# Rolling a matrix in HBM: 16 DMA engines placed 516 rows apart and a 128-column strip, where they stood 4 rows apart with a 256-column strip

## The chip, the cores and the metric

The kernel runs on one core of a Trainium2 chip. That core has 16 DMA engines, which move bytes between HBM and HBM and between HBM and the on-chip memory (SBUF). The metric is the device time of one launch in microseconds (us), given as the median of several runs; lower is better.

## The reference

```
x = np.random.randn(8192, 8192).astype(np.float32)      # 8192 rows of 32 KB
out = np.roll(x, 100, axis=1)
```

Each row is moved 100 columns to the right: `out[r, 100:] = x[r, :8092]`, and the last 100 columns of `x[r]` become `out[r, :100]`. Nothing is computed. All 268.4 MB are read once and written once.

## The kernel before, in words

The output is cut by columns. `s` is the shift, 100. `a` is the width of a strip at the left of the output: the shift rounded up to 128 columns, and then, by a rule of two lines (20 to 22), widened by another 128, so `a` is 256. `g = a - s` is 156: the first column of `x` that the strip does not take.

**The main part** (line 38) is `out[:, 256:] = x[:, 156:8092]`: 7936 columns, or 31,744 bytes of each row, copied from HBM to HBM with no stop on the chip. The rows go in blocks of 64. In block `c` there are four DMAs, `j` = 0 to 3; each has 16 rows, one for each DMA engine, and engine `e` takes row `64c + 4e + j`. So neighbouring engines are always 4 rows (128 KB) apart, all sixteen are in one block of 64 rows (2 MB), and one engine goes by 1 row three times and then 61 rows on, to its place in the next block. The DMAs are issued alternately by SyncE (SP: `j` = 0 and 2) and ScalarE (ACT: `j` = 1 and 3), 256 by each. Four DMAs of each queue are open at a time: the fifth waits until all 16 engines have finished the first.

**The strip** (lines 60 to 77) is the first 256 columns of the output, which cross the end of the rows in `x`. It goes through SBUF, with GpSimd (POOL) as issuer. The rows go in 4 stages of 2048 (`n_st`): 128 partitions of 16 consecutive rows, which are J = 4 groups of Q = 4 rows. Since row `r`'s last 100 columns and row `r+1`'s first columns are neighbours in HBM, one piece of 256 columns (1 KB) fetches both: for `q` = 1 to 3, line 68 reads the piece that begins 100 columns before row `q` of each group into the tile `t`. Line 69 fetches the last 100 columns of the fourth row (400-byte pieces), and line 72 the first 156 columns of the first row (624-byte pieces), straight into the tile `h`. VectorE (DVE) copies the other parts from `t` to `h` (lines 70 and 73). Then line 77 writes `h` out, one DMA for each `q` and stage: 512 pieces of 1 KB. In all there are 20 loads and 16 stores by POOL; eight may be open at a time, and the ninth waits for the first.

There are no waits between the main part and the strip: they share the 16 DMA engines, HBM, and nothing else. The Tile framework sets the semaphores; the order of each queue is that of the program.

Of the kernel before, what the change touches and what calls it, by code (L numbers as in the profile page):

```python
# [1 line left out]

# [4 lines left out]


@with_exitstack
def kernel(  # L10
    ctx: ExitStack,
    tc: tile.TileContext,
    x: bass.AP,
    shift: int,
    out: bass.AP,
):
    nc = tc.nc
    n_rows, n_cols = x.shape
    s = shift % n_cols
    a = -(-s // 128) * 128  # L20
    if 0 < a <= 384 and a + 128 <= n_cols:
        a += 128
    g = a - s
    P = nc.NUM_PARTITIONS
    engines = [nc.sync, nc.scalar]
    n_chunks = 16
    rows = n_rows // n_chunks

    xm = x.rearrange("(c e j) w -> c j e w", e=16, j=4)
    om = out.rearrange("(c e j) w -> c j e w", e=16, j=4)
    if a < n_cols:
        for c in range(n_rows // 64):
            for j in range(4):
                engines[j % 2].dma_start(out=om[c, j, :, a:], in_=xm[c, j, :, g:n_cols - s])
    if a == 0:
        return  # L40


    if a > 512:
        for i in range(n_chunks):
            r = slice(i * rows, (i + 1) * rows)
            nc.gpsimd.dma_start(out=out[r, :s], in_=x[r, n_cols - s:])
            if g > 0:
                nc.gpsimd.dma_start(out=out[r, s:a], in_=x[r, :g])
        return

    Q, J = 4, 4
    n_st = n_rows // (P * Q * J)
    reads = ctx.enter_context(tc.tile_pool(name="reads", bufs=n_st))
    heads = ctx.enter_context(tc.tile_pool(name="heads", bufs=n_st))
    xt = x.rearrange("(k p j q) c -> k q p j c", q=Q, j=J, p=P)
    ot = out.rearrange("(k p j q) c -> k q p j c", q=Q, j=J, p=P)  # L60
    tiles = []
    for k in range(n_st):
        t = reads.tile([P, Q - 1, J, a], x.dtype)
        h = heads.tile([P, Q, J, a], x.dtype)
        for q in range(1, Q):
            lead = bass.AP(tensor=x.tensor, offset=(k * P * J * Q + q) * n_cols - s,
                           ap=[[J * Q * n_cols, P], [Q * n_cols, J], [1, a]])
            nc.gpsimd.dma_start(out=t[:, q - 1], in_=lead)  # L68
        nc.gpsimd.dma_start(out=h[:, Q - 1, :, :s], in_=xt[k, Q - 1, :, :, n_cols - s:])  # L69
        nc.vector.tensor_copy(h[:, :Q - 1, :, :s], t[:, :, :, :s])  # L70
        if g > 0:
            nc.gpsimd.dma_start(out=h[:, 0, :, s:], in_=xt[k, 0, :, :, :g])  # L72
            nc.vector.tensor_copy(h[:, 1:, :, s:], t[:, :, :, s:])  # L73
        tiles.append(h)
    for k, h in enumerate(tiles):
        for q in range(Q):
            nc.gpsimd.dma_start(out=ot[k, q, :, :, :a], in_=h[:, q])  # L77


# [1 line left out]
_INS = ['x', 'shift']  # L81
_OUTS = [((8192, 8192), 'float32')]

_NUMBERS = {'shift': 100}


# [26 lines left out]
```

## Time and profile before

| | |
|---|---|
| median of 3 runs | 819.57 us (819.18 to 820.42) |
| the profiled execution, its own time | 820.42 us |
| its span, first to last instruction | 818.3 us |
| HBM read / written | 268.44 MB / 268.44 MB |
| moved by the DMA engines | 276.89 MB (strip bytes count twice: in and out) |
| main part, two queues | 2 x 130.04 MB |
| strip, one queue | 16.78 MB |
| last strip store issued | at 373.0 us |

In the profile, a DMA's packets carry their own times. For the main part a packet is one row (31,744 bytes), followed by a packet of 4 bytes that counts up a semaphore; so half of the packets of these two queues are rows. A strip packet is some 4 KB and holds several pieces: four of 1 KB, seven of 624 bytes, or ten or eleven of 400 bytes. The share of a queue is the time of its packets as a part of 16 engines' time in the window, so packet time can be had from a share: share x 16 x window / number of rows. Traffic on HBM in a window is twice the bytes of the main queues, which are read and written there, plus the strip queue's bytes, which touch HBM once.

### The profile page before, as it was taken

The page shows a single profiled execution, that of the slowest core. Times are in us where ns is not written, and L with a number is a line of the kernel's source. Part 1 is how long each engine was busy: PE and PEld are TensorE (multiplying, and loading weights), DVE is VectorE, ACT ScalarE, POOL GpSimd, SP SyncE. Part 2 cuts the span into 40 slices and gives each one's busy share as a digit, 9 for nine tenths or more (in the row PEclk, how much of TensorE's full clock was granted, in tenths as well). Part 3 has the DMA queues.
Part 4 walks back from the last instruction along what each step waited for, and adds up shares of the span by engine and source line. Part 5 has one row for each costly group of instructions (what it writes and reads, how often), then busy time and mean ns, then how long its engine had stood idle before and what let it go on. Part 6 is the DMA issues. An engine that isn't in the chain of part 4 may idle for free. (4 is left out here: it accounts for less than half of the span.)

```text
span 818.3 us, 617 instructions
## 1 busy us (share of the span) xinstructions
DVE 7.7 (1%) x8; POOL 28.8 (4%) x40
## 2 busy tenths in 40 slices
DVE  0000000000000000000000000000000000000000
POOL 3000000000000000000000000000000000000000
DMA  9999999999999999999999999999999999999997
GB/s 313 343 345 352 338 352 342 363 338 358 349 342 352 354 355 352 348 364 357 337 335 341 327 335 334 326 332 334 338 337 334 330 334 334 332 327 334 334 321 262
DMA packets 21060, 276.89 MB, mean 338 GB/s; under 512 B 8768, under 2 KB 8768, under 8 KB 12864
## 3 DMA queue, kind: packets, MB, share of 16 engines
q10 hardware_dynamic: 8192, 130.04, 46.4%
q1 hardware_dynamic: 8192, 130.04, 46.0%
q0 software_dynamic: 4672, 16.78, 6.8%
q14 instruction: 4, 0.03, 0.0%
HBM read 268.44 MB, written 268.44 MB: 656 GB/s over the span
## 5 line engine op out<-in xcount | busy, mean ns | idle before, releaser
L77 POOL DMA_DIRECT2D out_dram<-h x16 | 13.2, 825 | 197.8 <-DMA out_dram<-h 112.6
L68 POOL DMA_DIRECT2D t<-in_x_dram x12 | 9.5, 793 | 59.7 <-DMA h<-in_x_dram 30.0
L70 DVE COPY h<-t 128x1200 f32<-128x1200 f32 x4 | 3.1, 786 | 232.3 <-DMA t<-in_x_dram 173.4
L73 DVE COPY h<-t 128x1872 f32<-128x1872 f32 x4 | 4.9, 1224 | 0.0
L69 POOL DMA_DIRECT2D h<-in_x_dram x4 | 3.0, 748 | 45.4 <-DMA t<-in_x_dram 45.4
L72 POOL DMA_DIRECT2D h<-in_x_dram x4 | 3.0, 750 | 41.7 <-DMA t<-in_x_dram 41.7
L94 POOL MEMSET const-float32-0.0<- 128x1 f32 x1 | 0.1, 98 | 0.2 <-issue 0.2
L94 POOL MEMSET const-bfloat16-1.0<- 128x1 bf16 x1 | 0.1, 102 | 0.0
L94 POOL MEMSET const-uint8-127<- 128x1 uint8 x1 | 0.1, 99 | 0.0
L94 POOL MEMSET const-float32-1.0<- 128x1 f32 x1 | 0.1, 98 | 0.0
## 6 DMA issues: line engine op xcount, KB each, us to landing
out_dram<-in_x_dram ACTq DMA_DIRECT2D x256, 496.0 KB, 12.6
out_dram<-in_x_dram SPq DMA_DIRECT2D x256, 496.0 KB, 12.6
out_dram<-h POOLq DMA_DIRECT2D x16, 512.0 KB, 113.7
t<-in_x_dram POOLq DMA_DIRECT2D x12, 512.0 KB, 94.9
h<-in_x_dram POOLq DMA_DIRECT2D x4, 312.0 KB, 92.1
h<-in_x_dram POOLq DMA_DIRECT2D x4, 200.0 KB, 97.4
```

What stands on the lines that cost most here:

```text
L68: nc.gpsimd.dma_start(out=t[:, q - 1], in_=lead)
L69: nc.gpsimd.dma_start(out=h[:, Q - 1, :, :s], in_=xt[k, Q - 1, :, :, n_cols - s:])
L70: nc.vector.tensor_copy(h[:, :Q - 1, :, :s], t[:, :, :, :s])
L72: nc.gpsimd.dma_start(out=h[:, 0, :, s:], in_=xt[k, 0, :, :, :g])
L73: nc.vector.tensor_copy(h[:, 1:, :, s:], t[:, :, :, s:])
L77: nc.gpsimd.dma_start(out=ot[k, q, :, :, :a], in_=h[:, q])
L94: nc = _bacc.Bacc("TRN2", target_bir_lowering=False, num_devices=1)
```

## The change

The strip is 128 columns wide again: the rule of two lines is gone, so `a` = 128 and `g` = 28. J is 8, so the strip has 2 stages of 4096 rows and not 4 of 2048; its pieces are 512 bytes (and 400 and 112 bytes in `h`). The main part has 8064 columns, or 32,256 bytes, of each row.

The main part has a new order. `pitch` is 516 rows, `steps` is 7. A DMA still has 16 rows, one for each engine, but now engine `e` takes row `516e + 4q + 64i + j`. `j` runs fastest (1 row), then `i` from 0 to 6 (64 rows), then `q` from 0 to 15 (4 rows). This makes 448 DMAs. The rows that it leaves over are copied between `q` = 7 and `q` = 8: 60 DMAs of 16 rows that are 4 rows apart, as all were before, four of 15 rows, 516 apart, and four of a single row, which are cut into 16 parts of 504 columns (2016 bytes). That is 516 DMAs, 258 by each queue, where there were 512.

```diff
     a = -(-s // 128) * 128
-    if 0 < a <= 384 and a + 128 <= n_cols:
-        a += 128
     g = a - s
...
-    xm = x.rearrange("(c e j) w -> c j e w", e=16, j=4)
-    om = out.rearrange("(c e j) w -> c j e w", e=16, j=4)
+    pitch, steps = n_rows // 16 + 4, n_rows // 16 // 64 - 1
+    run = steps * 64
+
+    def main(n, first, step, count):
+        o = bass.AP(tensor=out.tensor, offset=first * n_cols + a, ap=[[step * n_cols, count], [1, n_cols - a]])
+        i = bass.AP(tensor=x.tensor, offset=first * n_cols + g, ap=[[step * n_cols, count], [1, n_cols - a]])
+        engines[n % 2].dma_start(out=o, in_=i)
+
     if a < n_cols:
-        for c in range(n_rows // 64):
-            for j in range(4):
-                engines[j % 2].dma_start(out=om[c, j, :, a:], in_=xm[c, j, :, g:n_cols - s])
+        for q in range(16):
+            for i in range(steps):
+                for j in range(4):
+                    main(j, 4 * q + 64 * i + j, pitch, 16)
+            if q == 7:
+                for e in range(15):
+                    for j in range(4):
+                        main(j, pitch * e + run + j, 4, 16)
+                for j in range(4):
+                    main(j, run + 64 + j, pitch, 15)
+                    main(j, n_rows - 4 + j, 1, 1)
...
-    Q, J = 4, 4
+    Q, J = 4, 8
     n_st = n_rows // (P * Q * J)
```

## The prediction

> **What bounds the kernel now.** I read the page's engine shares and DMA slices first, then its queues.
>
> ```profile
> span 818.3 us, 617 instructions
> DVE 7.7 (1%) x8; POOL 28.8 (4%) x40
> ...
> DMA  9999999999999999999999999999999999999997
> ...
> DMA packets 21060, 276.89 MB, mean 338 GB/s; under 512 B 8768, under 2 KB 8768, under 8 KB 12864
> ## 3 DMA queue, kind: packets, MB, share of 16 engines
> q10 hardware_dynamic: 8192, 130.04, 46.4%
> q1 hardware_dynamic: 8192, 130.04, 46.0%
> q0 software_dynamic: 4672, 16.78, 6.8%
> ...
> HBM read 268.44 MB, written 268.44 MB: 656 GB/s over the span
> ```
>
> No compute engine matters. The shares add up to 99.2% of 16 engines: the DMA engines always have a packet open. q10 and q1 are the main part, q0 the strip. A busy engine is not one at its full rate, though, so the next view is SP's own waits.
>
> ```profile
> SPq L38 <- DMA out_dram<-in_x_dram: 670.4, 252, 3.9
> ```
>
> 252 of SP's 256 issues waited, 670 us in all, for one of its four open DMAs. An issue itself takes 0.51 us, or 131 us in all. So the queues wait for the data, not the data for them. Then the DMA view of three stretches: strip loads (20 to 170 us), strip stores (240 to 360), main part alone (500 to 700).
>
> ```profile
> q10 hardware_dynamic: 1464, 23.27, 43.4%
> q1 hardware_dynamic: 1459, 23.11, 41.1%
> q0 software_dynamic: 1637, 5.79, 15.4%
> ```
>
> ```profile
> q1 hardware_dynamic: 1176, 18.67, 44.7%
> q10 hardware_dynamic: 1173, 18.54, 44.5%
> q0 software_dynamic: 1453, 5.28, 11.5%
> ```
>
> ```profile
> q1 hardware_dynamic: 2099, 33.34, 50.4%
> q10 hardware_dynamic: 2101, 33.37, 49.4%
> ```
>
> Bytes first, main part twice. Loads: (2 x 46.38 + 5.79) MB / 150 us = 657 GB/s on HBM. Stores: (2 x 37.21 + 5.28) / 120 = 664. Alone: 2 x 66.71 / 200 = 667. Now the time of one main row: 84.5% of 16 x 150 us over 1461 rows is 1388 ns beside the loads, 89.2% of 16 x 120 us over 1172 rows is 1461 ns beside the stores, and 99.8% of 16 x 200 us over 2101 rows is 1520 ns alone. When strip traffic comes in, main rows get faster by just so much that HBM traffic stays within 1.5%. The trace's fastest rows take 1174 ns, about a quarter of those in the last stretch. So what sets the end is the rate at which HBM serves these sixteen copies, some 667 GB/s, and not the DMA engines' own pace.
>
> **The strip, halved.** Every byte is still read from HBM once and written once: 536.87 MB before and after. What goes is the second handling by a DMA engine: the strip moves 8.39 MB and not 16.78, the main part 264.24 MB and not 260.08. Two ways of pricing that:
>
> By engine time, what the queues were charged is 99.2% of 818.3 us, 811.8 us. Strip: 6.8% of 818.3 is 55.6 us, halved 27.8. Main: 92.4% is 756.1 us; rows of 32,256 bytes for 31,744 add 1.6%, or 12.2. Sum -15.6 us. This end supposes that main rows keep their mean time per byte when the strip shrinks. The stretches show the opposite: without a strip a row takes 1520 ns, not 1388.
>
> By HBM traffic, the strip costs only what HBM loses while it runs. Loads: (667 - 657) / 667 x 150 us is 2.3 us for 5.79 MB, so 3.3 us for all 8.39 MB that are loaded. Stores: (667 - 664) / 667 x 120 us is 0.5 us for 5.28 MB, 0.8 for 8.39; the passage between the two (180 to 240 us, 649 GB/s by the same sum) makes it nearer 1.3. Together 4.6 us, and -2.3 when half of the bytes are gone. The other bound here: the number of pieces stays the same (8192 stored, one for each row, 1 KB before and 512 B after). If the loss goes by pieces, nothing is gained; if a 512-byte piece loses twice what a 1 KB piece does, +4.6. For it stands that the 400-byte pieces' packets took no longer per byte in the load stage than the 1 KB pieces' (284 ns for 4400 bytes, 267 for 4096, between 50 and 100 us of the trace). I take -2.3, by the row that it is nearest to, HBM's traffic; ends -15.6 and +4.6.
>
> POOL issues 10 loads and 8 stores in place of 20 and 16, of the same 512 KB (400 and 112 in `h`). Only two of the loads have to wait for one of the eight slots (12 did). DVE has four copies over 24 rows each for eight over 12. All of it hides: nobody in the main part waits for POOL or DVE, and strip work, of which the last store was issued at 373 us, should be issued by some 190 and landed by 250. If it were not, 550 us of main part are left as cover.
>
> **The new order of rows.** SP and ACT issue 258 DMAs each, +2 x 0.51 us, hidden in the 670 us of waits. The remainder in the middle: four DMAs of 15 rows leave one engine with four rows fewer, and four single rows add a 2016-byte part per engine. Sixteen engines wait for one at most: 4 rows x 1.5 us / 16 is 0.4 us. While these are open, a queue holds two real rows per engine, not four; DMAs land in 12.6 us with four open, so an engine that is 6 us ahead of the last can run dry once. Bound: 0 to 6 us; I take +0.4, since the other engines get HBM's free share.
>
> The spacing is the large unknown. Per engine, the sequence stays: 1, 1, 1, then 61 rows on; only each eighth jump differs. Between engines, 516 rows are 16 MiB + 128 KiB where there were 128 KiB; the 60 DMAs in the middle (12% of the rows) keep 4 rows. Modulo 512 rows the sixteen positions are the same as before. Nothing in this trace shows sixteen main rows 16 MiB apart. The nearest rows are those of the lone main part, a mean of 1520 ns in the 805 us from the first issue to the last. Ends: if all of them ran at the fastest, 1174 ns, the 805 us would be 622, -183 us; if all ran at the trace's 95th percentile, 2030 ns, on the 88% that are moved, +240 us. What the same kernel does from stretch to stretch, 649 to 667, is 2.7%. I take 0, because the positions modulo 512 rows stay, and because engines are not in step today (the first and the last engine of one DMA finish some 6 us apart, four rows), so no fixed pattern between them is there to be broken.
>
> A rule speaks against it: the Trainium skill, "DMA: Bandwidth & Descriptors", section "Latency and other measured facts", has HBM-to-HBM copies at half rate when streams lie 4 or 8 MiB apart, and full rate again with 4 KiB added to the pitch. By the rule without the padding, 88% of the rows at half rate would make some 1530 us; with the 128 KiB counted as padding, no change. No run here shows either. The other way, "HBM Reference", section "Specifications (TRN2)", gives a domain some 716 GB/s; 667 is 93% of that, so by this page even a perfect order would save 7% at most, to about 762 us.
>
> **Sum.** -2.3 + 0.4 = -1.9 us. Against the profiled execution's own 820.42 us (span 818.3 and 2.1 around it) that is 818.5; the median of the runs lies 0.85 below it, so 817.7 us.
>
> **The rivals.**
> 1. The spacing helps. For: three quarters of the lone main rows are slower than 1174 ns, so streams hinder each other, and regions 16 MiB apart may do so less. Against: 667 GB/s is hardly left in any stretch of 50 us (650 to 673). If HBM gains 2%, the 805 us lose 16 and the time is 802 us; at 1%, 810.
> 2. The spacing hurts (the other side). All rows 128 KiB apart lie in one stretch of 2 MB now; sixteen far regions may collide where neighbours did not. 3% on the moved 88% is 0.88 x 805 x 0.03 = 21 us: 839 us. It decides as soon as the mean main row is longer than its scaled 1520 x 1.016 = 1544 ns by 0.5%, at 1552.
> 3. The engines' time counts after all: -15.6 + 0.4, 804 us. For: 99% busy. Against: the rows' 1388, 1461 and 1520 ns.
> 4. 512-byte pieces cost HBM more: +4.6 + 0.4, 824.6 us. Against: the 400-byte packets.
>
> That the change doesn't do what it says, because the remainder's slots or the four-open window keep engines near each other, is out: positions are fixed by the addresses.
>
> **How the numbers follow.** Forecast 0.34, rival 1 0.22, rival 2 0.30, rival 3 0.07, rival 4 0.07. A change of under 0.2% (1.6 us) can't be told from none in this kernel. The forecast's own range is 814 to 820: half of its chance is faster, some 0.12 within 0.2%, 0.05 slower. So faster 0.17 + 0.22 + 0.07 = 0.46, same 0.12, slower 0.05 + 0.30 + 0.07 = 0.42. The range must reach into rivals 1 and 2: from 798 (HBM up by 2.5%) to 844 (3.7% on the moved rows), about one in ten left out on each side.
>
> **What the profile after would show.** Strip: q0 at 8.39 MB, its last store issued before 200 us. Forecast: HBM near 667 GB/s in a stretch of main part alone, rows near 1544 ns. Rival 1: rows below 1530. Rival 2: rows above 1552, and a dip of row time in the middle, where the 60 DMAs are 4 rows apart. Rival 3: rows at 1490 or less with q0 halved. Rival 4: less HBM traffic while the strip runs than 657, the rest unchanged. Wrong in any case if the slices show DMA gaps around the remainder.

## The result, and the profile after

The changed kernel takes 822.84 us (median of 4 runs, 822.02 to 823.95) where the kernel before took 819.38 in the same comparison: a ratio of 1.0043, with a 95% interval of 1.0025 to 1.0062. It is slower by 0.43%, some 3.5 us. The forecast was 817.7 us, faster by 0.23%: the time lies within the stated 798 to 844 us, a range wide enough for either sign, and the sign is wrong. The profiled execution took 822.36 us, with a span of 820.6.

The page of the changed kernel, its DMA slices and queues:

```profile
span 820.6 us, 593 instructions
DVE 3.7 (0%) x4; POOL 16.1 (2%) x22
...
DMA  9999999999999999999999999999999999999997
...
DMA packets 18845, 272.70 MB, mean 332 GB/s; under 512 B 8541, under 2 KB 8605, under 8 KB 10653
## 3 DMA queue, kind: packets, MB, share of 16 engines
q1 hardware_dynamic: 8252, 132.14, 47.6%
q10 hardware_dynamic: 8252, 132.14, 47.0%
q0 software_dynamic: 2336, 8.39, 4.4%
...
HBM read 268.44 MB, written 268.44 MB: 654 GB/s over the span
```

The bytes went as the change says: the strip's queue moves 8.39 MB and not 16.78, all engines together 272.70 MB and not 276.89. It won nothing. The engines are as busy as before and HBM's mean rate fell from 656 to 654 GB/s. This page shows best what kind of kernel it is: 4.2 MB less to move, and more time.

The DMA view of the strip's loads in the changed kernel (20 to 100 us), then of the main part alone (500 to 700 us); columns are packets, MB, share of 16 engines:

```profile
q1 hardware_dynamic: 762, 12.32, 40.9%
q10 hardware_dynamic: 754, 12.23, 39.6%
q0 software_dynamic: 761, 2.68, 19.9%
```

```profile
q1 hardware_dynamic: 2060, 33.36, 50.9%
q10 hardware_dynamic: 2054, 33.10, 49.4%
```

During the loads HBM carries (2 x 24.55 + 2.68) MB / 80 us = 647 GB/s, ten less than beside the 1 KB pieces (657). Alone it carries 2 x 66.46 / 200 = 665, where before had 667. Neither difference settles anything by itself, since single stretches of the same kernel differ by as much; the sizes below are therefore taken from timed ratios. By the sum of the prediction a main row of the last stretch takes 1560 ns (100.3% of 16 x 200 us over 2057 rows). That is above the 1552 ns that rival 2, the spacing hurts, had as its sign.

One place is plain, though. Stretches of 5 us in the middle of the changed kernel (columns: stretch, length, busy DVE, busy POOL, TensorE clock, DMA share, GB/s):

```profile
455.00:460.00 5.00, 0.00 (x0) 0.00 (x0) 1.00 1.00 336
460.00:465.00 5.00, 0.00 (x0) 0.00 (x0) 1.00 0.82 294
465.00:470.00 5.00, 0.00 (x0) 0.00 (x0) 1.00 0.94 338
470.00:475.00 5.00, 0.00 (x0) 0.00 (x0) 1.00 0.94 336
475.00:480.00 5.00, 0.00 (x0) 0.00 (x0) 1.00 1.01 310
```

Here the four DMAs of 15 rows and the four of a single row run. The DMA share falls to 0.82 and 0.94: (0.18 + 0.06 + 0.06) x 5 us is idle time worth 1.5 us of all 16 engines. A slice of the page is 20 us long, and in it this dip still counts as a 9.

### The profile page after: what moved, and what is told of

It reads as the page before. It is cut to its first block, busy times and chain, and to the rows that moved or that the text cites. A ratio compares the mean times of both kernels' runs of the same rounds, so it can differ in the third digit from the quotient of the medians.

```text
span 820.6 us, 593 instructions
## 1 busy us (share of the span) xinstructions
DVE 3.7 (0%) x4; POOL 16.1 (2%) x22
## 2 busy tenths in 40 slices
DMA packets 18845, 272.70 MB, mean 332 GB/s; under 512 B 8541, under 2 KB 8605, under 8 KB 10653
## 3 DMA queue, kind: packets, MB, share of 16 engines
q0 software_dynamic: 2336, 8.39, 4.4%
## 5 line engine op out<-in xcount | busy, mean ns | idle before, releaser
L90 POOL DMA_DIRECT2D out_dram<-h x8 | 6.9, 955 | 91.0 <-DMA h<-in_x_dram 78.9
L81 POOL DMA_DIRECT2D t<-in_x_dram x6 | 5.4, 910 | 0.8 <-PEq L121 0.8
L83 DVE COPY h<-t 128x2400 f32<-128x2400 f32 x2 | 2.8, 1410 | 115.1 <-DMA t<-in_x_dram 115.1
L85 POOL DMA_DIRECT2D h<-in_x_dram x2 | 1.8, 883 | 15.2 <-DMA t<-in_x_dram 15.2
L82 POOL DMA_DIRECT2D h<-in_x_dram x2 | 1.8, 882 | 14.8 <-DMA t<-in_x_dram 14.8
## 6 DMA issues: line engine op xcount, KB each, us to landing
out_dram<-in_x_dram ACTq DMA_DIRECT2D x254, 504.0 KB, 12.6
out_dram<-in_x_dram SPq DMA_DIRECT2D x254, 504.0 KB, 12.6
```

## The experiments

Three theories stood at the start: A, the 512-byte pieces of the strip cost HBM what was lost; B, rows 516 apart are served more slowly; C, engines run dry around the remainder's odd DMAs. The runs were spread over several chips, and these differ: the kernel before took between 821 and 833 us on them. So every ratio is one to the kernel before on the same chip, timed beside it, with its 95% interval.

### The strip alone

The order of before, the strip of after.

```diff
--- before
-    if 0 < a <= 384 and a + 128 <= n_cols:
-        a += 128
...
-    Q, J = 4, 4
+    Q, J = 4, 8
```

> The order of before (engines 4 rows apart, no remainder) with the 128-column strip of after. Theory A, the 512-byte pieces cost HBM what the change lost: 822 to 823 us, nothing of the loss is gone. Theory B, the 516-row spacing makes main rows slower: 817 to 818 us, the strip alone gains the 2.3 us of the forecast. Theory C, the loss is the remainder in the middle, where 15-row and single-row DMAs leave engines dry: also 817 to 818 us; the run with both new order and wide strip tells B from C.

Measured 833.92 us against 833.34: 1.0002 (0.9985 to 1.0019). Neither the 2.3 us gained of the forecast (0.9972) nor the loss of theory A (1.003 and more) lies in the interval. Taking half the bytes out of the strip is worth nothing that can be measured, and so A falls: the loss comes with the order of the rows.

### The order alone

After's order with before's strip (the two lines back, J = 4).

> The new order (516 rows, remainder in the middle) with the 256-column strip of before. A: 819.5 to 820.5 us, no loss but the remainder's. B: 823 us or more, with lone main rows 0.4% above 1520 ns. C: 821 us, with rows at 1520 ns and a dip around the remainder.

1.0076 (1.0052 to 1.0100). The whole loss, and rather more, with the wide strip. Its stretches around the odd DMAs have the same dip, deeper:

```profile
475.00:480.00 5.00, 0.00 (x0) 0.00 (x0) 1.00 0.75 262
480.00:485.00 5.00, 0.00 (x0) 0.00 (x0) 1.00 0.47 176
```

0.25 and 0.53 of 5 us are 3.9 us. The share of the next 5 us, 1.17, gives 0.9 of them back, because a packet's time is booked where it starts: some 3 us are left.

### The odd DMAs

First the imbalance alone was taken away: the DMAs of 15 rows are cut by columns, so that all 16 engines get the same; the single rows stay.

```diff
--- after
+                w = (n_cols - a) // 16
                 for j in range(4):
-                    main(j, run + 64 + j, pitch, 15)
+                    cut = [[w, 16], [pitch * n_cols, 15], [1, w]]
+                    r = (run + 64 + j) * n_cols
+                    engines[j % 2].dma_start(out=bass.AP(tensor=out.tensor, offset=r + a, ap=cut),
+                                             in_=bass.AP(tensor=x.tensor, offset=r + g, ap=cut))
                     main(j, n_rows - 4 + j, 1, 1)
```

> After, but the four 15-row DMAs of the remainder are cut into 16 column parts, so that all 16 engines get 15 parts of 2016 bytes. A and B: within 0.5 us of after, 822 to 823. C, as far as the missing engine is its cause: 1.5 us less, 821, and no dip in DMA busy share between 440 and 490 us.

1.0055 (1.0035 to 1.0074). The changed kernel was not timed on this chip; on two others it had 1.0043 and 1.0059, so nothing clear was won. The dip is still there:

```profile
465.00:470.00 5.00, 0.00 (x0) 0.00 (x0) 1.00 0.86 287
470.00:475.00 5.00, 0.00 (x0) 0.00 (x0) 1.00 0.91 299
475.00:480.00 5.00, 0.00 (x0) 0.00 (x0) 1.00 0.92 317
```

(0.14 + 0.09 + 0.08) x 5 us is some 1.5 us, as much as in the changed kernel. So the engine left out is not what makes the dip. The DMAs with little work still take places among the four open ones.

Then, on one chip: the changed kernel again, the same with the odd DMAs taken out of SP's and ACT's queues, and the odd DMAs put into before.

> The changed kernel itself, so that the others have it beside them on their chip. Both theories: 1.003 to 1.006 of before.

```diff
--- after
-    def main(n, first, step, count):
+    def main(n, first, step, count, by=None):
...
-        engines[n % 2].dma_start(out=o, in_=i)
+        (by or engines[n % 2]).dma_start(out=o, in_=i)
...
-                for j in range(4):
-                    main(j, run + 64 + j, pitch, 15)
-                    main(j, n_rows - 4 + j, 1, 1)
...
             nc.gpsimd.dma_start(out=ot[k, q, :, :, :a], in_=h[:, q])
+    for j in range(4):
+        main(j, run + 64 + j, pitch, 15, nc.gpsimd)
+        main(j, n_rows - 4 + j, 1, 1, nc.gpsimd)
```

> After, but the eight odd DMAs of the remainder (four of 15 rows, four of one row) are issued by POOL behind the strip's stores, so that SP's and ACT's windows of four always hold full rows. Theory C, the loss is the dry engines around the odd DMAs: the dip in the middle goes and the time falls to 0.999 to 1.001 of before. Theory B, the 516-row order itself slows HBM: the dip goes, 1.0 to 1.3 us are won, and 1.002 to 1.005 are left.

```diff
--- before
             for j in range(4):
-                engines[j % 2].dma_start(out=om[c, j, :, a:], in_=xm[c, j, :, g:n_cols - s])
+                for e in ([slice(0, 15), slice(15, 16)] if c == 64 else [slice(0, 16)]):
+                    engines[j % 2].dma_start(out=om[c, j, e, a:], in_=xm[c, j, e, g:n_cols - s])
```

> Before with nothing changed but one block of 64 rows in the middle, whose four DMAs of 16 rows are cut into 15 rows and 1 row each, as the remainder of after. C: a dip there of 10 to 20% over some 10 us, and 1.5 to 3.5 us more than before (1.002 to 1.004). B: 1.001 to 1.0015, what the idle engines of the dip come to.

| kernel | ratio to before | interval |
|---|---|---|
| changed kernel again | 1.0059 | 1.0042 to 1.0077 |
| odd DMAs by POOL | 1.0033 | 1.0017 to 1.0048 |
| before, with odd DMAs in the middle | 1.0023 | 1.0008 to 1.0037 |

Stretches of 5 us, the changed kernel on this chip, then the one with the odd DMAs issued by POOL:

```profile
460.00:465.00 5.00, 0.00 (x0) 0.00 (x0) 1.00 0.88 269
465.00:470.00 5.00, 0.00 (x0) 0.00 (x0) 1.00 0.72 254
```

```profile
460.00:465.00 5.00, 0.00 (x0) 0.00 (x0) 1.00 0.98 316
465.00:470.00 5.00, 0.00 (x0) 0.00 (x0) 1.00 1.04 348
```

And before with the odd DMAs put in:

```profile
420.00:425.00 5.00, 0.00 (x0) 0.00 (x0) 1.00 0.72 257
425.00:430.00 5.00, 0.00 (x0) 0.00 (x0) 1.00 0.65 227
```

The dip goes with the odd DMAs and comes with them. Issued by POOL they run earlier, beside the strip's stores, and make no dip there either (shares of 0.97 to 1.03 in stretches of 10 us from 120 to 230 us). Put alone into the old order they cost 1.9 us (0.23%, 0.7 to 3.0 us by the interval); taken out of the new one they give back 0.26% by the two ratios, whose intervals overlap a little. So theory C is true for something near half of the loss. The rest, 0.33%, stays when the dip is gone: theory B.

### The spacing

What it does to have engines exactly 512 rows (16 MiB) apart, with no remainder:

```diff
--- after
-    pitch, steps = n_rows // 16 + 4, n_rows // 16 // 64 - 1
+    pitch, steps = n_rows // 16, n_rows // 16 // 64
...
-            if q == 7:
...
```

> After with neighbouring engines exactly 512 rows (16 MiB) apart and therefore no remainder at all. If power-of-two pitches collide as the row of the Trainium skill's DMA page has it: rows at about twice their time, 1400 to 1600 us. If the 16 MiB bit and all above it are without effect, and engines are out of step: all engines lie in the same place modulo 16 MiB, and the time says what the 128 KiB offset is worth; A and B leave 822 us, C 820.5.

2595 us, 3.1 times before on the same chip and far above the 1400 to 1600 us that the power-of-two case was given. Its runs lie far apart (2389 to 2632 us); the record is of the slowest. The main part between 500 and 700 us:

```profile
q10 hardware_dynamic: 633, 10.10, 55.7%
q1 hardware_dynamic: 640, 10.32, 41.1%
q0 software_dynamic: 640, 2.36, 3.0%
```

96.8% of 16 x 200 us over 636 rows: a row takes 4870 ns in place of some 1560. Equal places modulo 16 MiB are a disaster; the four rows more (128 KiB) cure nearly all of it. The engines are nearly in step here, though: by the landing times in the record, the first and the last engine finish one DMA some 3.5 us apart, which is less than one row of this run (before and the changed kernel: some 6 us, four rows). So the run does not say what equal places cost engines that are rows apart. Next, an order that was meant to let a running engine and its neighbour meet all the time modulo 512 rows:

```diff
--- after
-        for q in range(16):
-            for i in range(steps):
+        for i in range(steps):
+            for q in range(16):
...
-            if q == 7:
+            if i == 3:
```

> After with q inside i: an engine goes through 64 rows one after the other before it jumps, so an engine that is four rows ahead is where its neighbour is, modulo 512 rows, all the time and not only at the 15 changes of q. If such meetings cost HBM time (B, by way of places modulo 512 rows, which the run at 512 rows speaks for): 2% or more above after. If not (C): as after within 0.2%.

1.0082 (1.0064 to 1.0100), 0.23% above the changed kernel and not 2%; the intervals overlap. That speaks against after's few changes of `q` as the rest of the loss. It does not exclude them, because in this record the engines of one DMA finish only some 4 us apart, two to three rows, so the meetings at four rows are rarer than the run was meant to make them. Then the cleanest form of the spacing: 508 rows, 4 less than 512, where all 512 DMAs have 16 full rows.

```diff
--- after, with the wide strip and with the narrow one
-    pitch, steps = n_rows // 16 + 4, n_rows // 16 // 64 - 1
+    pitch, steps = n_rows // 16 - 4, n_rows // 16 // 64 - 1
...
-                for e in range(15):
-                    for j in range(4):
-                        main(j, pitch * e + run + j, 4, 16)
-                for j in range(4):
-                    main(j, run + 64 + j, pitch, 15)
-                    main(j, n_rows - 4 + j, 1, 1)
+                for r in range(60):
+                    main(r, run + r, pitch, 16)
+                for j in range(4):
+                    main(j, n_rows - 64 + j, 4, 16)
```

> Before with only the order changed: neighbouring engines 508 rows apart (4 short of 512, as after's are 4 more), the 60 rows that each engine's region has left over copied at the same 508 rows apart, the last 64 rows in the order of before. All 512 DMAs have 16 full rows; no odd ones. Theory B, far regions in themselves cost HBM time: 1.003 to 1.006 of before. Theory D, the rest of the loss comes from after's remainder, 60 DMAs that jump from region to region: 1.000 to 1.0015.

> The same order with the 128-column strip of after. B: as the run with the wide strip within 0.2%, 1.003 to 1.006. D: 1.000 to 1.0015. If the strip's width matters beside the new order, though it didn't beside the old one, the two differ by more than 0.2%.

> Before's strip with after's order, and the eight odd DMAs issued by POOL. B: 1.003 to 1.006, as the 508-row run. D: the same 1.003 and more, but above the 508-row run by 0.2% or more. The narrow strip with the same order gave 1.0033.

508 rows with the wide strip 1.0058 (1.0037 to 1.0078), with the narrow one 1.0032 (1.0019 to 1.0045); 516 rows with the odd DMAs by POOL and the wide strip 1.0051 (1.0032 to 1.0071), beside 1.0033 with the narrow one above. With no odd DMA in SP's and ACT's queues at all, the order alone still costs 0.3 to 0.6%: theory B holds, and theory D, that the rest lies in after's remainder, does not. The order changes two things at once, though: how far engines are apart, and which block of 64 rows each engine takes next (six steps of one block on, then back). No run kept the engines 4 rows apart with just this succession, so the loss belongs to the two together. Whether the wide strip loses more beside this order stays open, as the intervals touch.

### What of the spacing costs

Whether a succession of blocks can cost time by itself is the next question. Four runs left engines 4 rows apart and only changed which block of 64 rows follows which.

```diff
--- before; the list is one of these four
-        for c in range(n_rows // 64):
+        for c in [8 * i + m for m in range(8) for i in range(16)]:
+        for c in [7 * i % 128 for i in range(128)]:
+        for c in [2 * i + m for m in range(2) for i in range(64)]:
+        for c in [63 * i % 128 for i in range(128)]:
```

> Before, but its blocks of 64 rows are visited 8 blocks (512 rows) apart, as after's remainder goes: engines stay 4 rows apart, only an engine that is ahead by a block is now 16 MiB and not 2 MiB on. D: 1.01 or more of before, since after has this on 12% of its rows and lost some 0.3%. B: 1.000 to 1.0015.

> Before, with its blocks of 64 rows visited 7 blocks (448 rows, 14 MiB) apart and not one after the other. Theory F, it costs HBM something whenever rows in flight lie in far regions, however far: 1.004 to 1.007, as the run with 512 rows. Theory G, the loss needs equal places modulo 512 rows (an engine ahead by a block then stands 16 MiB from the others, with the lower address bits alike): 1.000 to 1.0015.

> Before, with its blocks visited 2 apart (128 rows, 4 MiB): first all even ones, then all odd ones. F: 1.001 to 1.007; near 1.001 if distance counts by size, near 1.006 if any jump over a block does. G: 1.000 to 1.0015.

> Before, with its blocks visited 63 apart (4032 rows, 126 MiB), so that two regions half the matrix apart are in work at once. F: 1.004 to 1.008. G: 1.000 to 1.0015.

| blocks visited | ratio to before | interval |
|---|---|---|
| 512 rows apart | 1.0064 | 1.0047 to 1.0081 |
| 448 rows apart | 0.9997 | 0.9982 to 1.0013 |
| 128 rows apart | 1.0119 | 1.0098 to 1.0140 |
| 4032 rows apart | 1.0008 | 0.9991 to 1.0026 |

Distance as such (F) is out: 126 MiB costs nothing and 4 MiB costs 1.2%. G is out too, since 128 rows should have been harmless. What is left looks like even against odd numbers of blocks (H). That was put to engines 444 rows (7 blocks less 4 rows) and 124 rows (2 blocks less 4 rows) apart, all DMAs of 16 full rows, and to SP and ACT in two neighbouring blocks at once. The kernel with 124 rows has `2 * 64 - 4, 1` in the line shown, in each of four parts of 2048 rows; how both kernels copy the rows left over is not shown:

```diff
--- the kernel with 508 rows and the wide strip
-    pitch, steps = n_rows // 16 - 4, n_rows // 16 // 64 - 1
+    pitch, steps = 7 * 64 - 4, 6
...
--- before
-        for c in range(n_rows // 64):
+        for c in range(0, n_rows // 64, 2):
             for j in range(4):
-                engines[j % 2].dma_start(out=om[c, j, :, a:], in_=xm[c, j, :, g:n_cols - s])
+                for n in range(2):
+                    engines[n].dma_start(out=om[c + n, j, :, a:], in_=xm[c + n, j, :, g:n_cols - s])
```

> As the 508-row order with the wide strip, but neighbouring engines 444 rows (7 blocks less 4 rows) apart; the last 1088 rows in the order of before. Theory H, what costs is that rows in work at one time are an even number of 64-row blocks apart, above all powers of two (128 and 512 rows lost, 448 and 4032 did not): 0.9985 to 1.0015 of before. Theory F, far regions as such: 1.004 to 1.006, as the 508-row order. Nothing in either theory makes it faster.

> The same with neighbouring engines 124 rows (2 blocks less 4 rows) apart, in four parts of 2048 rows. H: a loss, since all engines are an even number of blocks apart; as the blocks visited 128 rows apart lost 1.2%, 1.005 to 1.015. F: the regions are nearer than 444 rows, so no more than that run.

> Before, but SP copies the even blocks of 64 rows and ACT the odd ones, side by side: the rows in work are always spread over two neighbouring blocks, which before they are only when an engine runs ahead. H, if an even mixture of even and odd blocks is good for HBM: 0.990 to 0.998 of before, a version that beats both kernels. If before is mixed well enough: 0.9985 to 1.0015.

444 rows: 1.0170 (1.0147 to 1.0194). 124 rows: 1.0191 (1.0167 to 1.0215). Two blocks at once: 1.0065 (1.0042 to 1.0088). H falls at the first: the odd spacing between engines is three to five times as costly as 508. The third, where an even mixture of blocks should have won, lost as well. The loss is rows served more slowly, with no engine idle. In the main part alone, 500 to 700 us, of the kernel with 444 rows and then of the one whose blocks go 4032 rows apart:

```profile
q1 hardware_dynamic: 2017, 32.07, 50.1%
q10 hardware_dynamic: 2017, 31.97, 49.9%
```

```profile
q1 hardware_dynamic: 2070, 32.76, 49.5%
q10 hardware_dynamic: 2069, 32.92, 49.5%
```

100.0% and 99.0% of the engines' time, and 64.04 MB against 65.68: 640 and 657 GB/s on HBM. On the chips of these two the kernel before took nearly the same time (830.79 and 831.27 us).

So this much is shown: no order tried is faster than the one of before. Leaving the 512 rows aside, the orders with engines 516, 508, 444 and 124 rows apart, the two blocks at once and two of the four other successions of blocks lose 0.3 to 1.9%. From 500 to 700 us their engines are as busy as those of before (98.9 to 100.3%, before 99.8), so the time goes into slower rows; only the order with `q` inside `i` has its odd DMAs in that stretch. Which address bits decide it was not found.

## Why the prediction was wrong

What bounds the kernel was right; all three terms of the sum were off, and to the same side. The step that failed most is the spacing, put at 0 and measured at 2.7 us. The strip's gain of 2.3 us did not come, and the remainder, put at 0.4 us, cost 1.9. That the time came within 0.6% of the forecast is no merit, as each of these terms is smaller than that.

**What bounds it: right.** HBM's rate sets the time, not the engines' own pace. Two things show it from the other side: 4.2 MB less for the DMA engines gave 1.0002, and the order of the same blocks alone gave up to 1.0119. Rival 3, -15.6 us by the engines' time, is excluded by far.

**The strip, -2.3 us: no gain measured.** Its other bound, that the loss goes by pieces and not by bytes, came nearer (0.0 us, with 1.5 either way). I had argued against it with the 400-byte pieces, whose packets seemed to take no longer per byte than those of 1 KB pieces. That reading failed. It rests on 34 packets of one short stretch (284 ns, with a standard error of 44); over 20 to 170 us of the same record 84 such packets took 313 ns where 4096 bytes in 1 KB pieces took 258, 13% more per byte. In the changed kernel a 4096-byte packet of eight 512-byte pieces took 345 ns where one of four 1 KB pieces took 267 before (50 to 100 us from the first packet). The other records agree: from 20 to 100 us these packets have a mean of 260 to 322 ns in every run with the wide strip and of 328 to 423 ns in every one with the narrow strip. That these longer packets are why nothing was won is argued and not shown, since packet time is the engines' and not HBM's. From 20 us to the last strip packet, HBM fell behind its rate of 500 to 760 us by 4.3 us in the record before and by 3.2 in the one after, too near each other for single records. The cause stays open. Rival 4, +4.6 for 512-byte pieces, is out as well.

**The remainder, +0.4 us within 0 to 6: the price was 1.9 us.** The mechanism was named (a queue holds two real rows per engine instead of four, and an engine that is ahead runs dry), but the value taken was that of the missing engine alone, 4 rows x 1.5 us / 16. The run with the even remainder kept the whole dip, so this part is not the cost; the odd DMAs in the old order brought a dip, and POOL's queue took it away, so the cost is what they do in the window of four. The skew of 6 us, which I had before me, should have been set against 12.6 us of landing for four DMAs: halve the open work, and by this estimate a skew of 6 us eats all of it.

**The spacing, 0: the price was 2.7 us (0.33% with the odd DMAs out of the way; 0.32 to 0.58% at 508 rows).** It is rival 2's side, far regions served more slowly, at an eighth of its price: 0.37% on the moved 88% of rows, not 3%. Of its two reasons, one holds: places modulo 512 rows matter, as engines at equal places took 3.1 times as long, and keeping them kept the loss small. The other fell: engines that are four rows out of step were said to have no pattern left to be broken. In the changed kernel they are as far out of step as before (some 6 us in both records) and keep their places modulo 512 rows, and the new order still cost something. The prediction also took an engine's own sequence as nearly unchanged. But each seventh jump, not each eighth, now goes back 383 rows, some six blocks, and the runs with other successions of blocks show that succession alone can cost up to 1.2%.

**The sum.** 0.0 + 1.9 + 2.7 is 4.6 us, 0.56%. Measured were 0.43% and, on a second chip, 0.59%. The forecast's -1.9 missed the three terms by 1.5 to 2.7 us each, all to the same side.

**The two rules.** The page "DMA: Bandwidth & Descriptors" ("Latency and other measured facts") was right to warn of pitches at powers of two: where it has half rate at 4 and 8 MiB, the rate here, at 16 MiB, was 0.32 of before. That padding cures the loss held to within some half a per cent, with 128 KiB; the 4 KiB of the page was not tried. The limit of "HBM Reference" agrees: in no record does the main part alone (500 to 700 us) come above the 667 GB/s of before, 93% of its 716.

## What to carry to other kernels

Where HBM's own rate is the bound, count HBM's bytes and not the DMA engines': halving the detour through SBUF was worth nothing here. When a queue may hold only a few DMAs, one with little work in it takes up as much of the window as a full one, so leftovers are better placed in another queue. A new address order should be priced with both signs: the present one may be near the best. And before a run is read as a test of engines out of step, look in its record whether they are.

## What the runs showed of the hardware that was not expected

- Sixteen HBM-to-HBM copies exactly 16 MiB apart took 3.1 times as long (4870 ns for a row in place of some 1560), and their engines finished one DMA within some 3.5 us, less than one row, where it is some 6 us and four rows in the kernel before; 128 KiB more brought it back to 1.004.
- With everything else alike, the succession of blocks of 64 rows (2 MiB) changes the time: blocks 4 MiB apart cost 1.2%, 16 MiB 0.6%, 14 and 126 MiB nothing measurable.
- Packets of 512-byte loads took longer per byte than those of 1 KB loads (345 and 267 ns for 4096 bytes beside the main part), and half of the strip's bytes gave no time back (1.0002).
- The chips differ by 1.5% for the same kernel (821 and 833 us), three times the effect that was measured here.
